# Feed-forward up projections with tokens on the partitions of their sums, and the hidden values transposed for the down projection

## The chip, the cores and the metric

One core of a Trainium2 chip runs the whole program. The metric is the device time of one execution in microseconds, as the median of three runs. The engines are named as in the profile: PE is TensorE (its matmuls; PEld are its loads of the stationary operand), DVE is VectorE, ACT is ScalarE, POOL is GpSimd, SP is SyncE, which issues the weight loads.

## The reference

A trunk of two layers on 256 tokens of width 2048, all in float32. Layer 0 has a recurrent mixer (a matrix memory beside a gated linear recurrence), layer 1 a dilated attention of 16 heads. Each layer ends with the block that this case is about; the hidden width is 5632.

```python
def rmsnorm(x, g):
    y = xf * lax.rsqrt(jnp.mean(jnp.square(xf), axis=-1, keepdims=True) + RMS_EPS)
    return (y * g.astype(jnp.float32)).astype(x.dtype)

def swiglu(h, w1, w3, w2):
    return (jax.nn.silu(h @ w1) * (h @ w3)) @ w2
...
        h = rmsnorm(x, f_norm[l])
        x = x + swiglu(h, f_w1[l], f_w3[l], f_w2[l]).astype(x.dtype)
    return rmsnorm(x, final_norm)
```

## The kernel before, in words

**Exact products out of parts.** Every float32 operand is written as the sum of two parts of type float32r: the rounded value, made by an ACT copy, and the rest, made by a DVE subtraction (`split2` for results, `emit_split` for weights, lines 204 and 205). A product takes three of the four products of parts: high by high, high by low, low by high.

**The weight stream.** All weights come in items of 1 MB, [128, 4, 512], loaded by SP into four buffers `raw`. Each item makes two steps of [128, 2, 512], that is of eight blocks of 128 x 128 weights. For each step ACT writes `wh` and DVE `wl`, four buffers each, three steps (AHEAD) ahead of the products. `emit_step` issues the products of one step to PE, then lets the background tasks run one turn (`run_tasks`). An evacuation (the handling of a finished sum) is a generator in the list `urgent`, which is advanced by one `yield` in every turn. `lag()` waits one turn more (LAG = 1), so that operands made by other engines are there when PE gets to the instruction.

**Two forms of product.** In the *narrow* form (`add_chunk`, `narrow`, lines 272 to 274) the activations are the stationary operand and the weights stream: for each block of 128 features and each of two tiles of 128 tokens there are three matmuls of 512 columns, one for each pair of parts, into a bank `acc` of [128 tokens, 512 outputs]. A step has two feature blocks, so 12 matmuls; a chunk of 512 outputs takes two banks. In the *wide* form (`add_blocks`, lines 294 and 295) the weights are stationary and the activations stream: for each block of 128 x 128 weights one matmul of 512 columns (the high weights by both parts of 256 tokens side by side) and one of 256 columns (the low weights by the high activations). Its sum, [128 outputs, 512], takes one bank, whose two halves `join` adds; units of 128 outputs come in pairs.

**Norms.** The residual `xres` has tokens on the partitions. `norm_evac` adds a chunk of a projection to it, takes the squares, transposes it with PE (`transpose`, line 141, tile `nT`) and writes `xT`, [feature, token] in two parts, times the norm's gains. The norm's own factors, one per token, are applied to the results: `cur["rstd"]` has them for tokens on the partitions; `rstd_rows` spreads them along the free axis into `rb` by two products with ones (line 331), which wide results need.

**The feed-forward block** (`ffn`, lines 921 to 981). The hidden width is 44 blocks of 128, done in two parts (`UPS`): 24 blocks and their down projection, then 20 and theirs. The up projections are wide; units of w1 and w3 alternate. For each block, `up1` joins the w1 sum, multiplies it by `rb` and takes Silu; `up3` joins the w3 sum, multiplies it by `rb` and by the other, and splits the result into the tile `hT`, [hidden, token], four blocks to a tile of the slots. An up stretch is thus 96 or 80 steps. The down projection is narrow, with `hT` as the stationary operand: four chunks of outputs, each over all the hidden blocks of the part.

**Memory.** PSUM: four banks `acc`, two `tp` for transposes, two `mx`. SBUF: six buffers `ev` of [128, 512], eight slots of 8 KB (`hT`, the residual, the attention's tiles, the final gains), used in turn. POOL issues the few other loads and takes the norms' powers; the load of the final gains (`load_fg`) is issued 90 steps before the end.

Of the kernel before, what the change touches and what calls it, by code (L numbers as in the profile page):

```python
# [16 lines left out]
S = 256  # L17
# [19 lines left out]
# buffers: weights as loaded, their float32r parts and how many steps these run ahead  # L37
# [3 lines left out]
# work tiles of 8, 2 and 4 KB per partition  # L41
# [4 lines left out]
# background tasks at a time; stages that a product waits after its operands are issued  # L46
CONC = 3
LAG = 1
# products on constants that bring the tensor engine to its full clock before the data is there
WARM = 13  # L50
# step of the weights' parts from which the first norm is taken up
RS0 = 9
# column groups of the first layer's input projection, in the order of their products
# [11 lines left out]
def trunk_kernel(ctx: ExitStack, tc: tile.TileContext, a, out):  # L65
# [42 lines left out]
    def lag():  # L108
        """For operands of other engines to be ready when the tensor engine gets there."""
        for _ in range(LAG):  # L110
            yield

    def take():
        """One task at a time keeps a bank of mx (and one of tp) from stage to stage."""
        while held["mx"]:
            yield
        held["mx"] = True
# [11 lines left out]
    # ---------------------------------------------------------------- consts  # L129
# [16 lines left out]
    # ------------------------------------------------------ the weight stream  # L146
# [4 lines left out]
    def load_xT(k0, n):  # L151
        """Feature blocks of the transposed input, [feature, token]."""
        i, r = divmod(k0, 8)
        if i not in x_in:
            x_in[i] = slot((8, S), name="xin")
        SP.dma_start(x_in[i][:, r:r + n, :], a["xT"][:, k0:k0 + n, :])
# [34 lines left out]
    def emit_split(s):  # L191
        """Weights of step s into float32r parts."""
        st = steps[s]
        it = st["item"]
        raw = loaded[it][:, 2 * st["half"]:2 * st["half"] + 2, :]
        hi = whp.tile([P, 2, CW], F32R, tag="wh", name="wh")
        lo = wlp.tile([P, 2, CW], F32R, tag="wl", name="wl")
        for k in (0, 1) if s < 2 else (slice(0, 2),):
            if s < 2:
                use_xT(2 * s + k)  # L200
            elif s < KB // 2:
                use_xT(2 * s)
                use_xT(2 * s + 1)
            A.copy(hi[:, k], raw[:, k])  # L204
            V.tensor_tensor(lo[:, k], raw[:, k], hi[:, k].bitcast(F32), op=ALU.subtract)  # L205
        splits[s] = (hi, lo)
        if st["last_half"]:
            loaded.pop(it)
            emit_load()

    def add_unit(src, ch, kb0, first, last, act):
        """Four blocks of features by 512 outputs; tokens on the outputs' partitions."""
        items.append(wload(src, len(items)))
        it = len(items) - 1
        for h in range(2):
            steps.append({
                "item": it, "half": h, "last_half": h == 1, "ch": ch, "kb": kb0 + 2 * h, "act": act,
                "first": first and h == 0, "last": last and h == 1, "wide": False, "before": None,
            })
# [7 lines left out]
    def add_blocks(units):  # L227
        """Units of 128 outputs on the outputs' partitions: (weights, act, evac), two at a time."""
        for i in range(0, len(units), 2):
            pair = []  # L230
            for src, act, evac in units[i:i + 2]:
                items.append(wload(src, len(items)))
                pair.append((len(items) - 1, Chunk(evac), act))
            for h in range(2):
                for it, ch, act in pair:
                    steps.append({
                        "item": it, "half": h, "last_half": h == 1, "ch": ch, "kb": 8 * h, "act": act,
                        "first": h == 0, "last": h == 1, "wide": True, "before": None,
                    })
# [65 lines left out]
    # ------------------------------------------------------------- shared bits  # L305
# [5 lines left out]
    def split2(dst, src):  # L311
        """Exact float32r parts of src into dst [.., 2, S]."""
        A.copy(dst[:, 0, :], src)  # L313
        V.tensor_tensor(dst[:, 1, :], src, dst[:, 0, :].bitcast(F32), op=ALU.subtract)  # L314

    def join(acc, dst):
        """Both column halves of a wide unit's sum, times the tokens' norm factors."""
        A.copy(dst, acc[:, S:])  # L318
        V.tensor_tensor(dst, acc[:, :S], dst, op=ALU.add)  # L319

    def rstd_rows(r):
        """The norm factors along the free axis on every partition."""
# [15 lines left out]
    def norm_evac(n, gains, ssq, xt, last=False):  # L338
        """Adds the chunk to the residual; its transpose, times the gains, for the next products."""

        def gen(ch):
# [35 lines left out]
            if n == NCD - 1:  # L377
                r = const.tile([P, 2], F32, name=f"rstd{gains}")
                V.tensor_reduce(r, ssq, axis=mybir.AxisListType.X, op=ALU.add)
                V.tensor_scalar(r, r, 1.0 / D, EPS, op0=ALU.mult, op1=ALU.add)  # L380
                power(r, r, 2)
                yield
                yield from rstd_rows(r)
                cur["rstd"] = r
                flags.add(f"rstd{gains}")
# [11 lines left out]
    # ================================================================ layer 0  # L397
    # ---- recurrent block: conv, gates and scans in [channel, time]
# [44 lines left out]
    def rg_scan(c, wt):  # L443
        """Two channel blocks, both directions."""
# [18 lines left out]
        # 1 - a^2 = tanh(-log a) (1 + a^2)  # L463
# [50 lines left out]
    # ---- matrix memory: both directions in their quadratic form  # L514
    ml, ys = {}, {}

    def gates_task():
# [39 lines left out]
        # log sigmoid of the forget gates beside softplus(-lam): min(z, 0) - ln(1 + exp(-|z|))  # L557
# [8 lines left out]
        # half of -8 softplus(-lam) = 8 log sigmoid(lam)  # L566
# [6 lines left out]
        # cumulated forget gates, [token, direction * head]  # L573
# [57 lines left out]
    def qk_block(i, h):  # L631
        """q (i = 0, scaled) or k of a head, [feature, token]."""
# [174 lines left out]
    # the residual, two tiles of two chunks  # L807
# [8 lines left out]
    # ================================================================ layer 1  # L816
    at = {}

    def att_qk(i, h):
        """Minus the scaled q (i = 0) or k of a head, [feature, token], in float32r parts."""  # L820
# [38 lines left out]
    def mm3(o, lhs, rhs, start, stop):  # L859
        """One product of float32 operands out of their float32r parts."""  # L860
# [59 lines left out]
    # ==================================================================== ffn  # L920
    def ffn(l, gains, nxt):
# [3 lines left out]
        def up1(f):  # L925
            def gen(ch):
                st["e", f] = e = ev("up")
                while f"rstd{gains}" not in flags:
                    yield
                t = e[:, :S]  # L930
                join(ch.acc[0], t)
                ch.acc = None
                V.tensor_tensor(t, t, cur["rB"], op=ALU.mult)  # L933
                A.activation(t, t, AF.Silu)  # L934
                flags.add(f"up{l}_{f}")
# [4 lines left out]
        def up3(f, f0):  # L940
            def gen(ch):
                while f"up{l}_{f}" not in flags:
                    yield
                e = st.pop(("e", f))
                t = e[:, S:]
                join(ch.acc[0], t)
                ch.acc = None
                V.tensor_tensor(t, t, cur["rB"], op=ALU.mult)
                if (f - f0) % 4 == 0:
                    st["h", f] = slot((4, 2, S), F32R, name="hT")  # L950
                V.tensor_tensor(t, t, e[:, :S], op=ALU.mult)  # L951
                split2(st["h", f - (f - f0) % 4][:, (f - f0) % 4], t)
                flags.add(f"h{l}_{f}")
                yield

            return gen

        def act_h(kb):
            until(f"h{l}_{kb}")
            return st["h", kb // 4 * 4][:, kb % 4]  # L960

        for hidx, (c0, c1) in enumerate(UPS):
            units = []
            for f in range(4 * c0, 4 * c1):
                units += [(a["w1"][l, f], act, up1(f)), (a["w3"][l, f], act, up3(f, 4 * c0))]
            add_blocks(units)
# [16 lines left out]
    # ============================================================ the program  # L983
# [21 lines left out]
    def first_rstd():  # L1005
        """The input's sums of squares, out of its transpose."""
# [47 lines left out]
    def out_proj(w, gains, act, name, order):  # L1054
        """The first two chunks leave the operands that come last for later."""
# [42 lines left out]
    # ------------------------- the last products and the final norm, by tokens  # L1098
# [26 lines left out]
# ---- layout on the host  # L1125
def tiled(w):
    """[K, N] into [N / 512, K / 512, 128, 4, 512]: one contiguous piece per load."""
# [4 lines left out]
def blocks(w):  # L1132
    """[2048, N] into [N / 128, 128, 4, 512]: all the rows of 128 outputs per load."""
# [8 lines left out]
def constants():  # L1142
    """What depends on the shapes alone."""
# [13 lines left out]
def arrange(x, e_norm, e_w_in, e_gate_b, e_conv_w, e_conv_b, e_rg_wa, e_rg_ba, e_rg_wx, e_rg_bx,  # L1157
# [25 lines left out]
        "w1": np.stack([blocks(f_w1[l]) for l in range(2)]),  # L1183
        "w3": np.stack([blocks(f_w3[l]) for l in range(2)]),
# [20 lines left out]
```

## Time and profile before

| what | value |
|---|---|
| median of three runs | 2259.32 us (2259.19 to 2259.65) |
| span of the profiled execution, first to last instruction | 2256.9 us |
| median less span (start and end of an execution) | 2.4 us |
| mean granted TensorE clock over the span | 0.999 |
| PE / PEld busy | 2240.3 / 1903.8 us (99% / 84%) |
| DVE busy | 1391.3 us (62%) |
| ACT busy | 1097.7 us (49%) |
| weights and all else read from HBM | 414.09 MB, 184 GB/s over the span |
| up stretches, layer 0 | 373.84 to 646.49 and 778.90 to 1005.03 us |
| up stretches, layer 1 | 1510.03 to 1782.66 and 1914.98 to 2138.27 us |

The profile is of one execution. Busy time of an engine is the union of its instructions' times; matmuls overlap one another, so a count times a mean duration is more than the busy time, and what one of them costs in a row is the distance from its start to the start of the next. The chain is followed back from the last instruction, at each step to what released it. In rows of groups the columns are the line, engine, operation, output tile and input tiles, shapes and count, then busy time, the mean duration in ns, and the engine's idle time before them with what ended it.

### The profile page before, as it was taken

What the parts mean: (1) busy time and instruction counts of PE and PEld (TensorE: products, weight loads), DVE (VectorE), ACT (ScalarE), POOL (GpSimd) and SP (SyncE); (2) the same over time, 40 slices, a digit from 0 to 9 for tenths busy, and PEclk for the clock granted to TensorE, in tenths of its full rate; (3) what the DMA queues carried; (4) which work ended last, traced back from release to release, by engine and by line L of the source; (5) the groups of instructions that cost most, each with busy time, mean ns of one, the idle gap of its engine ahead of it and who ended that gap; (6) DMA issues with size and microseconds to landing.
All of it is one profiled execution on the core that took longest, in us unless ns stands there. A gap on an engine that the chain in (4) does not pass through costs nothing.

```text
span 2256.9 us, 29286 instructions
## 1 busy us (share of the span) xinstructions
PE 2240.3 (99%) x11660; PEld 1903.8 (84%) x11660; DVE 1391.3 (62%) x1960; ACT 1097.7 (49%) x1603; POOL 23.8 (1%) x42
## 2 busy tenths in 40 slices
PE   9999999999999999999999999999999999999998
PEld 7878888888888888888888888888888888888886
DVE  6867856666654466665566676556666544666654
ACT  5667545444443344444454554454444433444443
POOL 1000000000000000000000000000000000000000
PEclk9999999999999999999999999999999999999999
DMA  7534655555555555555555555445555555555553
GB/s 289 182 122 151 221 171 187 187 187 186 187 186 189 184 187 187 187 193 182 191 190 176 186 183 175 168 171 185 185 187 187 204 187 202 191 189 189 192 196 112
DMA packets 61354, 418.09 MB, mean 185 GB/s; under 512 B 6972, under 2 KB 7628, under 8 KB 12448
## 3 DMA queue, kind: packets, MB, share of 16 engines
q1 hardware_dynamic: 58176, 406.35, 52.1%
q0 software_dynamic: 2608, 9.26, 1.2%
q8 instruction: 91, 1.49, 0.3%
q10 hardware_dynamic: 432, 0.60, 0.1%
q14 instruction: 47, 0.39, 0.0%
HBM read 414.09 MB, written 2.10 MB: 184 GB/s over the span
## 4 chain that ended last, share of the span: by engine, by line
PE 95%; DVE 2%; ACT 1%; issue 1%; DMA 0%; SPq 0%; POOL 0%; POOLq 0%; DVEq 0%; ACTq 0%
PE acc L294 37%; PE acc L295 19%; PE acc L272 12%; PE acc L274 12%; PE acc L273 12%; DVE wl L205 1%; PE rgp L454 1%; ACT wh L204 1%; PE nT L141 0%; DVE xc L421 0%; DMA raw<-in_w_v 0%; PE apT L141 0%; PE num L724 0%; PE asc L862 0%; PE apo L861 0%
## 5 line engine op out<-in xcount | busy, mean ns | idle before, releaser
L205 DVE TENSOR_TENSOR wl<-raw,wh 128x1024 fp32r<-128x1024 f32 (+1 forms) x770 | 932.8, 1221 | 727.2 <-ACT wh L204 698.7
L294 PE MATMUL acc<-xT,wh 128*128 128x512 f32 x3712 | 1314.8, 396 | 0.4 <-ACT v L662 0.4
L204 ACT CAST wh<-raw 128x1024 fp32r<-128x1024 f32 (+1 forms) x770 | 802.0, 1044 | 568.3 <-PE acc L274 324.1
L295 PE MATMUL acc<-xT,wl 128*128 128x256 f32 x3712 | 1045.1, 282 | 0.0
L294 PEld LDWEIGHTS acc<-xT,wh 128*128 128x128 f32 x3712 | 697.8, 188 | 165.5 <-ACT v L662 0.6
L295 PEld LDWEIGHTS acc<-xT,wl 128*128 128x128 f32 x3712 | 696.8, 188 | 1.1 <-DVE wl L205 0.3
L272 PE MATMUL acc<-wh,hT 128*128 128x512 f32 x704 | 276.9, 393 | 0.0
L274 PE MATMUL acc<-wh,hT 128*128 128x512 f32 x704 | 275.9, 392 | 0.0
L273 PE MATMUL acc<-wl,hT 128*128 128x512 f32 x704 | 275.7, 392 | 0.0
L274 PEld LDWEIGHTS acc<-wh,hT 128*128 128x128 f32 x704 | 132.2, 188 | 29.9
L273 PEld LDWEIGHTS acc<-wl,hT 128*128 128x128 f32 x704 | 132.4, 188 | 29.0
L272 PEld LDWEIGHTS acc<-wh,hT 128*128 128x128 f32 x704 | 132.3, 188 | 28.8
L313 ACT CAST hT<-up 128x256 fp32r<-128x256 f32 x88 | 35.8, 406 | 198.7 <-DVE up L951 198.7
L934 ACT ACTIVATE up<-up 128x256 f32<-128x256 f32 x88 | 36.8, 418 | 157.8 <-DVE up L933 157.8
L272 PE MATMUL acc<-wh,xT 128*128 128x512 f32 x256 | 104.1, 407 | 0.5 <-ACT wh L204 0.5
L273 PE MATMUL acc<-wl,xT 128*128 128x512 f32 x256 | 101.3, 396 | 1.0 <-DVE wl L205 1.0
L274 PE MATMUL acc<-wh,xT 128*128 128x512 f32 x256 | 101.1, 395 | 0.0
L319 DVE TENSOR_TENSOR up<-acc,up 128x256 f32<-128x256 f32 x176 | 73.5, 418 | 1.5 <-ACT up L318 1.5
L318 ACT COPY up<-acc 128x256 f32<-128x256 f32 x176 | 64.2, 365 | 0.0
L314 DVE TENSOR_TENSOR hT<-up,hT 128x256 fp32r<-128x256 f32 x88 | 37.4, 426 | 41.6 <-ACT hT L313 41.6
L272 PEld LDWEIGHTS acc<-wh,xT 128*128 128x128 f32 x256 | 48.1, 188 | 12.5 <-ACT wh L204 1.5
L273 PEld LDWEIGHTS acc<-wl,xT 128*128 128x128 f32 x256 | 48.1, 188 | 11.8 <-DVE wl L205 1.6
(228 smaller groups left out, 1371.3 us busy)
## 6 DMA issues: line engine op xcount, KB each, us to landing
raw<-in_w SPq DMA_DIRECT2D x264, 1024.0 KB, 4.8
raw<-in_w_aqk SPq DMA_DIRECT2D x32, 1024.0 KB, 4.9
raw<-in_w_out SPq DMA_DIRECT2D x16, 1024.0 KB, 4.8
raw<-in_w_av SPq DMA_DIRECT2D x16, 1024.0 KB, 4.8
raw<-in_w_o SPq DMA_DIRECT2D x16, 1024.0 KB, 4.8
raw<-in_w_xr SPq DMA_DIRECT2D x8, 1024.0 KB, 8.6
raw<-in_w_qk SPq DMA_DIRECT2D x8, 1024.0 KB, 4.9
raw<-in_w_og SPq DMA_DIRECT2D x8, 1024.0 KB, 4.8
```

The source lines that it names most:

```text
L204: A.copy(hi[:, k], raw[:, k])
L205: V.tensor_tensor(lo[:, k], raw[:, k], hi[:, k].bitcast(F32), op=ALU.subtract)
L272: PE.matmul(acc, xh, hi[:, j, :], start=f, stop=False)
L273: PE.matmul(acc, xh, lo[:, j, :], start=False, stop=False)
L274: PE.matmul(acc, xl, hi[:, j, :], start=False, stop=e)
L294: PE.matmul(acc, wh[:, j, :], x2.rearrange("p a b -> p (a b)"), start=f, stop=False)
L295: PE.matmul(acc[:, :S], wl[:, j, :], x2[:, 0, :], start=False, stop=e)
L313: A.copy(dst[:, 0, :], src)
L314: V.tensor_tensor(dst[:, 1, :], src, dst[:, 0, :].bitcast(F32), op=ALU.subtract)
L318: A.copy(dst, acc[:, S:])
L319: V.tensor_tensor(dst, acc[:, :S], dst, op=ALU.add)
L934: A.activation(t, t, AF.Silu)
```

## The change

Up projections use the narrow form. w1 and w3 are laid out in memory in chunks of 512 outputs as the other narrow weights are (`tiled` in place of `blocks`), and each chunk of w1 is followed by the same chunk of w3. `up1` takes Silu straight out of the two banks, with the norm's factor as the scale of each partition; `up3` multiplies the w3 banks by the factor and by that, in place. The result has tokens on the partitions, in two `ev` tiles of [128, 512]; two turns later 8 PE transposes in two groups of four (tile `hTp`, in the `tp` banks) bring it to [hidden, token], one group in each of two turns, and each group is split into `hT` out of PSUM. The two norms ahead of feed-forward blocks no longer run `rstd_rows`. The names, the down projections, the buffers and the other products stay. Comments and docstrings go as well.

```diff
@@ norm_evac @@
                 power(r, r, 2)
-                yield
-                yield from rstd_rows(r)
                 cur["rstd"] = r
+                if gains == G_O:
+                    yield
+                    yield from rstd_rows(r)
                 flags.add(f"rstd{gains}")
@@ ffn @@
-        def up1(f):
+        def up1(c):
             def gen(ch):
-                st["e", f] = e = ev("up")
                 while f"rstd{gains}" not in flags:
                     yield
-                t = e[:, :S]
-                join(ch.acc[0], t)
+                es = []
+                for t in range(2):
+                    e = ev("up")
+                    A.activation(e, ch.acc[t], AF.Silu, scale=cur["rstd"][:, t:t + 1])
+                    es.append(e)
                 ch.acc = None
-                V.tensor_tensor(t, t, cur["rB"], op=ALU.mult)
-                A.activation(t, t, AF.Silu)
-                flags.add(f"up{l}_{f}")
+                st["e", c] = es
+                flags.add(f"up{l}_{c}")
                 yield
...
-        def up3(f, f0):
+        def up3(c):
             def gen(ch):
-                while f"up{l}_{f}" not in flags:
+                while f"up{l}_{c}" not in flags:
                     yield
-                e = st.pop(("e", f))
-                t = e[:, S:]
-                join(ch.acc[0], t)
+                es = st.pop(("e", c))
+                for t in range(2):
+                    V.scalar_tensor_tensor(
+                        es[t], ch.acc[t], cur["rstd"][:, t:t + 1], es[t], op0=ALU.mult, op1=ALU.mult
+                    )
                 ch.acc = None
-                V.tensor_tensor(t, t, cur["rB"], op=ALU.mult)
-                if (f - f0) % 4 == 0:
-                    st["h", f] = slot((4, 2, S), F32R, name="hT")
-                V.tensor_tensor(t, t, e[:, :S], op=ALU.mult)
-                split2(st["h", f - (f - f0) % 4][:, (f - f0) % 4], t)
-                flags.add(f"h{l}_{f}")
                 yield
+                yield from lag()
+                h = st["h", c] = slot((4, 2, S), F32R, name="hT")
+                for p in range(2):
+                    ps = tp("hTp")
+                    for k in range(2):
+                        f0 = (2 * p + k) * P
+                        for t in range(2):
+                            transpose(ps[:, k, t * P:(t + 1) * P], es[t][:, f0:f0 + P])
+                    A.copy(h[:, 2 * p:2 * p + 2, 0, :], ps)
+                    V.tensor_tensor(
+                        h[:, 2 * p:2 * p + 2, 1, :], ps, h[:, 2 * p:2 * p + 2, 0, :].bitcast(F32), op=ALU.subtract
+                    )
+                    for k in range(2):
+                        flags.add(f"h{l}_{4 * c + 2 * p + k}")
+                    yield
...
         for hidx, (c0, c1) in enumerate(UPS):
-            units = []
-            for f in range(4 * c0, 4 * c1):
-                units += [(a["w1"][l, f], act, up1(f)), (a["w3"][l, f], act, up3(f, 4 * c0))]
-            add_blocks(units)
+            for c in range(c0, c1):
+                add_chunk(a["w1"][l, c], 4, act, up1(c))
+                add_chunk(a["w3"][l, c], 4, act, up3(c))
@@ arrange @@
-        "w1": np.stack([blocks(f_w1[l]) for l in range(2)]),
-        "w3": np.stack([blocks(f_w3[l]) for l in range(2)]),
+        "w1": np.stack([tiled(f_w1[l]) for l in range(2)]),
+        "w3": np.stack([tiled(f_w3[l]) for l in range(2)]),
```

More of the change, by code (lines that the diff above doesn't have):

```diff
@@ L959, in act_h @@
             until(f"h{l}_{kb}")
-            return st["h", kb // 4 * 4][:, kb % 4]
+            return st["h", kb // 4][:, kb % 4]
         for hidx, (c0, c1) in enumerate(UPS):
-            units = []
-            for f in range(4 * c0, 4 * c1):
-                units += [(a["w1"][l, f], act, up1(f)), (a["w3"][l, f], act, up3(f, 4 * c0))]
-            add_blocks(units)
+            for c in range(c0, c1):
+                add_chunk(a["w1"][l, c], 4, act, up1(c))
+                add_chunk(a["w3"][l, c], 4, act, up3(c))
             if hidx == 1:
```

## The prediction

> **What bounds the kernel now.** I read the page first (share of the engines, the chain that ended last, the costliest groups), then the busy time in the four stretches that the change touches, then the chain piece by piece there.
>
> ```profile
> span 2256.9 us, 29286 instructions
> PE 2240.3 (99%) x11660; PEld 1903.8 (84%) x11660; DVE 1391.3 (62%) x1960; ACT 1097.7 (49%) x1603; POOL 23.8 (1%) x42
> ...
> PE 95%; DVE 2%; ACT 1%; issue 1%; DMA 0%; SPq 0%; POOL 0%; POOLq 0%; DVEq 0%; ACTq 0%
> ...
> L205 DVE TENSOR_TENSOR wl<-raw,wh 128x1024 fp32r<-128x1024 f32 (+1 forms) x770 | 932.8, 1221 | 727.2 <-ACT wh L204 698.7
> L294 PE MATMUL acc<-xT,wh 128*128 128x512 f32 x3712 | 1314.8, 396 | 0.4 <-ACT v L662 0.4
> L204 ACT CAST wh<-raw 128x1024 fp32r<-128x1024 f32 (+1 forms) x770 | 802.0, 1044 | 568.3 <-PE acc L274 324.1
> L295 PE MATMUL acc<-xT,wl 128*128 128x256 f32 x3712 | 1045.1, 282 | 0.0
> ```
>
> The reader is to see that TensorE (PE) sets the time: 95% of the chain, and the wide products' lines 294 and 295 hardly ever wait. DVE and ACT mostly wait for each other and for PE to free the buffers of the weights' parts. A time of 396 ns is that of one matmul from start to end; they overlap, so costs here go by start to start. The four up stretches, with the sums of all engines:
>
> ```profile
> core 0: us, PE busy (x) PEld busy (x) DVE busy (x) ACT busy (x) POOL busy (x), PEclk, DMA share, GB/s
> 373.84:646.49 272.65, 272.65 (x1550) 237.71 (x1549) 174.22 (x247) 131.60 (x198) 0.72 (x1) 1.00 0.55 188
> 778.90:1005.03 226.13, 226.13 (x1282) 197.08 (x1281) 143.00 (x198) 106.06 (x157) 0.00 (x0) 1.00 0.55 189
> 1510.03:1782.66 272.63, 272.63 (x1550) 237.60 (x1548) 174.26 (x247) 131.66 (x198) 0.71 (x1) 1.00 0.55 188
> 1914.98:2138.27 223.29, 223.29 (x1281) 195.56 (x1280) 142.90 (x197) 105.64 (x157) 0.00 (x0) 1.00 0.56 191
> sum 994.70, PE 994.70 PEld 867.96 DVE 634.37 ACT 474.97 POOL 1.44; mean PE 248.68 PEld 216.99 DVE 158.59 ACT 118.74 POOL 0.36
> ```
>
> PE is busy in every microsecond of these 994.70 us, at the full clock. They are 96 + 80 + 96 + 80 = 352 steps of 8 weight blocks (128 x 128), 2816 blocks. The second stretch holds products alone: 226.13 / 640 = 353.3 ns a block, one matmul of 512 columns and one of 256, as the chain shows:
>
> ```profile
> 779.76 0.24 PE acc L294
> 780.00 0.12 PE acc L295
> 780.12 0.23 PE acc L294
> ```
>
> So only what changes PE's own work counts, unless PE is made to wait.
>
> **The change, part by part.** *Up products.* A narrow step covers the same 8 blocks with 2 feature blocks x 2 token tiles x 3 matmuls = 12 of 512 columns, 1.5 a block instead of 512 + 256. The columns are equal (768 a block); a quarter of the instructions goes. The products that already do exactly this, with xT as the stationary operand, are those of the first attention group (36 matmuls from 1133.18 on, in the stretch below) and of the next three (23 intervals in each):
>
> ```profile
> 1133.18:1141.58 8.40, 8.40 (x38) 1.00 0.37 125
> 1200.38:1205.74 5.36, 5.36 (x25) 1.00 0.58 196
> 1275.03:1280.39 5.36, 5.36 (x26) 1.00 0.59 196
> 1349.88:1355.26 5.38, 5.38 (x26) 1.00 0.59 196
> ```
>
> (The counts take in one or two that overlap the edges.) 8.40 / 36 = 233.3 ns each; the others give 233.0, 233.0 and 233.9. The same line with hT as the stationary operand isn't always as slow; 24 matmuls on the second and on the third hT tile of a down projection, in its second pass and again in its fourth:
>
> ```profile
> 685.10:690.55 5.45, 5.45 (x26) 1.00 0.53 189
> 690.55:696.15 5.60, 5.60 (x26) 1.00 0.59 202
> 751.30:756.75 5.45, 5.45 (x26) 1.00 0.54 188
> 756.75:762.35 5.60, 5.60 (x26) 1.00 0.55 199
> ```
>
> 227.1 and 233.3 ns, and both come back at the same tile in each pass: the rate goes with the stationary tile, not with chance. The up products' tile is xT, so I take 233.3 ns, and keep 227.1 as the low end. 352 x 12 = 4224 matmuls x 233.3 = 985.5 us.
>
> The Trainium skill, in "TensorE: Matmul & The Clock Gate" (Back-to-back issue gap), gives N / 2.4 + 2.5 ns at full clock, so a fixed cost of 2.5 ns for each matmul; by that half a matmul fewer per block would save an estimated 2816 x 0.5 x 2.5 = 3.5 us in all. The rows above show more for each matmul (233.3 ns for 512 columns), and they decide.
>
> *Transposes.* New on PE: 22 chunks of 512 outputs x 8 = 176 transposes of 128 x 128, in 44 groups of four. The nearest are those of the norm, which also stand between narrow steps (chain; below them eight at the start of an up stretch, and the products of rstd_rows):
>
> ```profile
> 1492.44 0.23 PE acc L274
> 1492.67 0.44 PE nT L141 x4
> 1493.10 0.24 PE acc L272
> ```
>
> ```profile
> 1512.99 0.87 PE nT L141 x8
> ...
> 1522.33 0.44 PE rbp L331 x4
> ```
>
> 44 x 0.44 = 19.4 us, all on the path: PE has no idle time there that could take it. Bounds from other rows of the same operation, and one for a wait of it on DVE:
>
> ```profile
> L141 PE MATMUL nT<-cst,xres x96: 270/272/328, 326.2 to 1513.6; 128*128 128x128 f32 x96
> ...
>   DVE xres L345: 1.2, 4
> ```
>
> Low 0.42 a group (half of 0.87, less a rounding); high 0.44 + 0.30, if each group waited for its input as those four did (1.2 / 4): 32.6 us.
>
> *Norm factors along the rows.* For the two feed-forward norms rstd_rows goes (its wait for the PE broadcast, one DVE copy): the L331 row, 2 x 0.44 = 0.9 us saved.
>
> *The sum.* Before: 994.7, of it 2 x 0.87 norm transposes, which stay. After: 985.5 + 1.7 + 19.4 = 1006.6. Difference +11.9 us.
>
> *Evacuations* (no cost). Beside the weights' parts (352 x 1.221 = 430 us DVE, 352 x 1.044 = 367 ACT, from the groups above) DVE now spends 204 us and ACT 107 on results. Nearest rows to the new operations:
>
> ```profile
> L849 ACT ACTIVATE av<-acc,rstd 128x512 fp32r<-128x512 f32 x8 | 5.0, 682 | 0.0
> L850 DVE SCALAR_TENSOR_TENSOR av<-acc,rstd,av 128x512 fp32r<-128x512 f32 x8 | 5.6, 743 | 0.0
> L313 ACT CAST apv<-apT 128x512 fp32r<-128x512 f32 x16 | 9.4, 585 | 11.8 <-PE apT L141 11.7
> L314 DVE TENSOR_TENSOR apv<-apT,apv 128x512 fp32r<-128x512 f32 x16 | 10.9, 684 | 7.5 <-ACT apv L313 7.5
> ```
>
> A chunk takes 2 x 0.743 + 2 x 0.684 = 2.9 us of DVE and 2 x 0.682 + 2 x 0.585 = 2.5 of ACT; times 22, 63 and 56 us. Both fall, and as neither bounds, this is worth nothing: where one reads 634 us of DVE, 141 go and PE stays.
>
> *New waits.* up3 multiplies in the task turn after the step that follows its last one; the transposes of the first half come two turns later, those of the second three: 2 x 2.80 us in which DVE has to do 2 x 0.743 and its weight parts (1.22 a step). If that cover went, PE would stand before the transpose and the whole queue of products behind it. Then ACT's copy of the transposes waits for PE with the next weight casts behind it; these run three steps (8.4 us) ahead, against 0.585 + 1.04 + 1.22. Nothing.
>
> *Banks, buffers, queues.* A chunk takes two accumulators of four, free again when the next but one begins: 8 steps for evacuations of 1.4 us. The loads are as many and as large; SP issues one for every two steps, now in the order of use, a step being 2.80 instead of 2.83 us: nothing. POOL loses no instruction; its load of the final gains takes its slot one hT tile earlier, so that one tile changes place: 96 matmuls x 6.2 ns, 0.6 us either way.
>
> All of it is against the profiled execution, whose span is 2256.9; the median of the runs, 2259.3, is 2.4 more (start and end, unchanged). **2259.3 + 11.9 = 2271.2 us**, 0.5% slower.
>
> **Rivals.**
> *Quicker products (the other side).* If w1 and w3 as the moving operand meet xT in the quicker pattern of some hT tiles, a matmul takes 227.1: 4224 x 6.2 ns = 26 us less, 2245. It decides from 230.5 ns down (11.9 / 4224 = 2.8 less), where the time is that of before. For it: the fourth stretch above does the second's work in 2.8 us less, so a rhythm can differ with the same tiles. Against: xT is at 233.0 to 233.9 in all four groups. At the middle of the hT tiles, (227.1 + 233.3) / 2 = 230.2, it is no change: 2258.
> *The transposes wait.* 0.30 us in each of 44 groups: +13.2, 2284. For it: those four; against: they had one turn, these have two.
> *Transposes that don't overlap.* At 272 ns each (their whole duration), 176 take 47.9 us instead of 19.4: 2300. Against: 0.44 us for four in the chain. The Trainium skill, same page, Part 4 (PE-mode transpose), speaks of about 275 ns for one in a kernel's context; the trace agrees as to duration (272), not as to spacing (110).
> *It does not do what it says* can't be: the instructions themselves change.
>
> **How the numbers follow.** Forecast 74%: own range 2268 (233.0 ns, 1.3 us less; 0.42 a group, 0.9 less; the one tile's 0.6) to 2275 (233.9 ns, 2.5 more, and the 0.6, rounded up). Quicker products 16%, half of it beyond -0.2%, half between; waiting transposes 8%; not overlapping 2%. A measurement here tells about 0.2% (4.5 us) from no change. So faster 8%, same 8%, slower 84%. The range is 2256 to 2284: down to the middle hT rate with the hT tile's 0.6 and a microsecond of rounding, up to the waiting transposes; the 227.1 case and the last rival stay out.
>
> **What would show it.** Up stretches of 96 steps take about 274.0 us (268.8 + 0.87 + 10 x 0.44) instead of 272.6, those of 80 steps 227.5 (224.0 + 8 x 0.44), and the last two groups of each stand in the down projection behind it; narrow products on xT at 233 ns start to start; 176 hTp transposes in pieces of 0.44 us in the chain; DVE about 1250 us busy, ACT about 1047; no PE wait for es, accumulators or wl. I am wrong if xT's matmuls fall below 231 ns, or if PE stands idle at the chunks' seams.

## The result, and the profile after

The changed kernel takes 2271.28 us (median of five runs, 2270.73 to 2271.55), the kernel before 2259.32 (2258.72 to 2259.65): a ratio of 1.0052, 95% interval 1.0041 to 1.0064. That is 12.0 us slower, where 11.9 were forecast.

The page of the changed kernel, its span, its busy times and its chain:

```profile
span 2269.0 us, 25922 instructions
PE 2251.6 (99%) x10420; PEld 1846.6 (81%) x10420; DVE 1248.0 (55%) x1514; ACT 1042.9 (46%) x1339; POOL 23.8 (1%) x42
...
PE 95%; DVE 2%; ACT 1%; issue 1%; DMA 1%; POOL 0%; POOLq 0%; DVEq 0%; SPq 0%; ACTq 0%
PE acc L272 26%; PE acc L273 26%; PE acc L274 26%; PE acc L294 8%; PE acc L295 4%; PE hTp L141 1%; DVE wl L205 1%; PE rgp L455 1%; ACT wh L204 1%; DMA raw<-in_w_v 1%; PE nT L141 0%; DVE xc L422 0%; PE apT L141 0%; PE num L725 0%; PE asc L863 0%
```

PE is still 95% of the chain. Its instructions fell by 1240 and its time rose; DVE lost 143 us of work and ACT 55, and the time took no notice of either. The four up stretches after, with the same columns as before the change:

```profile
374.24:648.24 274.00, 274.00 (x1201) 221.12 (x1200) 134.02 (x124) 116.53 (x127) 0.72 (x1) 1.00 0.55 185
781.53:1008.99 227.46, 227.46 (x993) 183.62 (x992) 110.06 (x98) 93.55 (x98) 0.00 (x0) 1.00 0.55 185
1514.77:1788.78 274.01, 274.01 (x1202) 220.22 (x1200) 134.07 (x124) 116.45 (x127) 0.71 (x1) 1.00 0.54 185
1922.11:2149.59 227.48, 227.48 (x994) 183.62 (x993) 110.05 (x98) 93.62 (x98) 0.00 (x0) 1.00 0.55 185
sum 1002.95, PE 1002.95 PEld 808.58 DVE 488.20 ACT 420.14 POOL 1.43; mean PE 250.74 PEld 202.15 DVE 122.05 ACT 105.03 POOL 0.36
```

994.70 became 1002.95: 8.2 us more. The first three down projections, after and then before, in one sum each:

```profile
sum 380.33, PE 380.33; mean PE 126.78
```

```profile
sum 377.55, PE 377.55; mean PE 125.85
```

Each takes 0.9 us more, the two groups of transposes of the last chunk ahead of it (2 x 0.44). With the fourth (119.4 after, 118.7 before, from its first product to the end of the span) that is 3.5 us. The rest of the 12.1 us between the spans is at the start: the first long weight load lands a little later (after, then before; pieces of the chain, start, us, what):

```profile
5.26 7.50 DMA raw<-in_w_v
```

```profile
4.97 7.34 DMA raw<-in_w_v
```

In the other runs of either form it lands anywhere from 12.1 to 13.1 us, so this is scatter and not the edited lines; here it is worth 0.4 us.

### The profile page after: what moved, and what is told of

Read it like the earlier page. It is cut to its first block, busy times and chain, and to the rows that moved or that the text cites. A ratio compares the mean times of both kernels' runs of the same rounds, so it can differ in the third digit from the quotient of the medians.

```text
span 2269.0 us, 25922 instructions
## 1 busy us (share of the span) xinstructions
PE 2251.6 (99%) x10420; PEld 1846.6 (81%) x10420; DVE 1248.0 (55%) x1514; ACT 1042.9 (46%) x1339; POOL 23.8 (1%) x42
## 4 chain that ended last, share of the span: by engine, by line
PE 95%; DVE 2%; ACT 1%; issue 1%; DMA 1%; POOL 0%; POOLq 0%; DVEq 0%; SPq 0%; ACTq 0%
PE acc L272 26%; PE acc L273 26%; PE acc L274 26%; PE acc L294 8%; PE acc L295 4%; PE hTp L141 1%; DVE wl L205 1%; PE rgp L455 1%; ACT wh L204 1%; DMA raw<-in_w_v 1%; PE nT L141 0%; DVE xc L422 0%; PE apT L141 0%; PE num L725 0%; PE asc L863 0%
## 5 line engine op out<-in xcount | busy, mean ns | idle before, releaser
L272 PE MATMUL acc<-wh,xT 128*128 128x512 f32 x1664 | 663.8, 399 | 0.9 <-ACT wh L204 0.8
L273 PE MATMUL acc<-wl,xT 128*128 128x512 f32 x1664 | 657.5, 395 | 1.2 <-DVE wl L205 1.2
L274 PE MATMUL acc<-wh,xT 128*128 128x512 f32 x1664 | 657.2, 395 | 0.0
L274 PEld LDWEIGHTS acc<-wh,xT 128*128 128x128 f32 x1664 | 312.4, 188 | 75.9
L272 PEld LDWEIGHTS acc<-wh,xT 128*128 128x128 f32 x1664 | 312.4, 188 | 75.7 <-ACT wh L204 2.0
L273 PEld LDWEIGHTS acc<-wl,xT 128*128 128x128 f32 x1664 | 312.5, 188 | 74.7 <-DVE wl L205 2.2
L294 PE MATMUL acc<-xT,wh 128*128 128x512 f32 x896 | 322.0, 400 | 0.4 <-ACT v L663 0.4
L295 PE MATMUL acc<-xT,wl 128*128 128x256 f32 x896 | 252.2, 281 | 0.0
L294 PEld LDWEIGHTS acc<-xT,wh 128*128 128x128 f32 x896 | 168.5, 188 | 38.9 <-ACT v L663 0.5
L295 PEld LDWEIGHTS acc<-xT,wl 128*128 128x128 f32 x896 | 168.2, 188 | 0.9 <-DVE wl L205 0.3
L964 DVE TENSOR_TENSOR hT<-hTp,hT 128x512 fp32r<-128x512 f32 x44 | 30.4, 691 | 57.1 <-ACT hT L963 57.1
L272 PE MATMUL acc<-wh,oT 128*128 128x512 f32 x128 | 51.0, 398 | 0.0
L274 PE MATMUL acc<-wh,oT 128*128 128x512 f32 x128 | 50.3, 393 | 0.0
```

Of the source, the lines that this page charges most:

```text
L272: PE.matmul(acc, xh, hi[:, j, :], start=f, stop=False)
L273: PE.matmul(acc, xh, lo[:, j, :], start=False, stop=False)
L274: PE.matmul(acc, xl, hi[:, j, :], start=False, stop=e)
L294: PE.matmul(acc, wh[:, j, :], x2.rearrange("p a b -> p (a b)"), start=f, stop=False)
L295: PE.matmul(acc[:, :S], wl[:, j, :], x2[:, 0, :], start=False, stop=e)
L964: V.tensor_tensor(h[:, 2 * p:2 * p + 2, 1, :], ps, h[:, 2 * p:2 * p + 2, 0, :].bitcast(F32), op=ALU.subtract)
```

## Experiments

**What the two terms are worth by themselves.** The transposes are left out.

```diff
-                    ps = tp("hTp")
-                    for k in range(2):
-                        f0 = (2 * p + k) * P
-                        for t in range(2):
-                            transpose(ps[:, k, t * P:(t + 1) * P], es[t][:, f0:f0 + P])
+                    ps = es[p].rearrange("q (k s) -> q k s", k=2)
```

> The changed kernel with the 176 transposes left out: the split into hT reads the two up tiles from SBUF instead of the transposes' bank, so the hidden values are in the wrong places; every other instruction stays. Theory (the two terms of the sum are what was worked out): 44 x 0.44 = 19.4 us less than the changed kernel, 2251.9 us, that is 7.4 us less than before; the up stretches take 269.6 and 224.0 us. Rival (the products themselves are slower in the narrow form by what chunks' seams and evacuations cost, and the transposes fill gaps): less than 10 us go and the time stays above 2259.

Measured: 2251.53 us, ratio to before 0.9967 (0.9955 to 0.9980). Its up stretches (us, PE busy, count, granted clock, DMA share, GB/s):

```profile
374.54:644.21 269.67, 269.67 (x1161) 1.00 0.53 187
776.73:1000.72 223.99, 223.99 (x961) 1.00 0.53 188
1505.72:1775.39 269.67, 269.67 (x1161) 1.00 0.53 187
1907.72:2131.71 223.99, 223.99 (x961) 1.00 0.54 188
sum 987.32, PE 987.32; mean PE 246.83
```

223.99 / 960 = 233.3 ns a matmul, in a stretch of nothing but products. Without its transposes the changed form is therefore quicker than the wide one in the up stretches, by 994.7 - 987.3 = 7.4 us: 0.9 of it is the two `rstd_rows` that went, 6.5 the products. The transposes cost 1002.95 - 987.32 = 15.6 us in the up stretches, which hold 36 of the 44 groups, 0.43 a group. The whole times say the same: 12.0 us above the kernel before with them, 7.4 below it without (2258.92, measured along with this run), so 19.4 us for the 44. Both terms stand as they were worked out, and the rival (transposes in gaps) falls.

**What sets 227 or 233 ns.** The prediction took the rate from the stationary tile, without a reason for it. The places of the tiles in the compiled program suggest one. Bytes within a partition: `xT` begins at 25440, the `wh` buffers at 92192 and every 4096 on, `wl` at 108576 and every 4096, the slots at 137248 and every 8256. The low and the high weights are thus alike modulo 256, and so are all the stationary pieces of one tile (512 bytes apart). The distance (the place of the stationary tile less that of the weights' parts, modulo 256) is 64 for xT; for the hT tiles of the first down projection it is 192, 0, 64, 0, 192, 128. Two tiles are in the prediction (the second, 227.1 ns, at 0; the third, 233.3 ns, at 64); here are the first (192) and the sixth (128), 24 matmuls each, before the change:

```profile
679.60:685.10 5.50, 5.50 (x26) 1.00 0.54 183
707.12:712.70 5.58, 5.58 (x26) 1.00 0.53 186
```

229.2 and 232.5 ns. That gave the theory of the next four runs: the distance decides, 227.1 ns at 0, 233.3 at 64, 232.6 at 128, 229.2 at 192. First 64 bytes behind xT:

```diff
     xT = const.tile([P, KB, 2, S], F32R, name="xT")
+    const.tile([P, 16], F32, name="pad")
```

> The changed kernel with 64 bytes of unused memory a partition behind xT, so that the weights' parts, and all behind them, lie 64 bytes further: the distance from the weights' parts to xT becomes a multiple of 256 bytes (it was 64 more than one). Theory (the rate of a narrow matmul goes with the distance, modulo 256 bytes, of the stationary tile from the weights that stream: 227 ns at 0, 233.3 at 64, 232.6 at 128, 229.2 at 192, as the hT tiles show): xT's matmuls fall to 227 ns; 4224 x 6.3 = 26.6 us from the up products and 768 x 6.3 = 4.8 from the other narrow products on xT, so about 2240 us; the hT tiles keep their rates as they move along. Rival 1 (the rate belongs to the tile's own address): xT has not moved, 233.3 ns and 2271 us, while the hT tiles change their rates. Rival 2 (it belongs to the data or to the stage): nothing changes.

Measured: 2242.26 us, ratio to before 0.9926 (0.9912 to 0.9939), about 29 us less than the changed kernel from a tile that nobody uses.

```profile
372.03:638.99 266.96, 266.96 (x1201) 1.00 0.55 189
772.33:993.90 221.57, 221.57 (x994) 1.00 0.55 189
1498.41:1765.39 266.98, 266.98 (x1201) 1.00 0.55 189
1898.66:2120.23 221.57, 221.57 (x993) 1.00 0.55 190
sum 977.08, PE 977.08; mean PE 244.27
```

An up stretch of 80 steps holds 960 matmuls and 8 groups of transposes: (221.57 - 8 x 0.44) / 960 = 227.1 ns. The second and the third hT tile of the first down projection moved along with the weights' parts and kept their rates, in the second pass 227.1 and 233.3 ns:

```profile
678.52:683.97 5.45, 5.45 (x25) 1.00 0.55 182
683.97:689.57 5.60, 5.60 (x25) 1.00 0.54 195
```

To part the distance from the tile's own address, the unused tile was put ahead of xT, with 48 columns, so that all moved together:

```diff
+    const.tile([P, 48], F32, name="pad")
     xT = const.tile([P, KB, 2, S], F32R, name="xT")
```

> The changed kernel with 192 bytes of unused memory ahead of xT: xT, the weights' parts and all behind them move by 192 bytes, and every distance stays; xT comes to an address that is 32 more than a multiple of 256, as that of the quick hT tile was. Theory (distance): 233.3 ns on xT, 2271 us. Rival 1 (own address): 227 ns on xT, about 2240 us. Rival 2 (data or stage): 2271 us.

Measured: 2271.06 us; the second up stretch:

```profile
781.81:1009.32 227.51, 227.51 (x994) 1.00 0.54 185
```

233.3 ns, as without the edit, though every address moved. The own address is out, and with the run before it the data and the stage are out too. The other two distances (32 and 48 columns behind xT):

> The changed kernel with 128 unused bytes behind xT: distance 192 modulo 256 from the weights' parts to xT, and the slots move along with the weights' parts. Theory (the distance decides, by the table read from the hT tiles): 229.2 ns, 4.1 less for 4224 + 768 narrow products on xT, 20.5 us, so 2250.8. Rival (only distance 0 is quick, all others alike): 2271.

> The changed kernel with 192 unused bytes behind xT: distance 128. Theory: 232.6 ns, 0.7 less for 4992 products, 3.5 us, so 2267.8. Rival (the farther the quicker, half of 256 being the farthest): less than 229 ns, below 2250.

Measured: 2252.36 us at 192 and 2267.22 us at 128; the second up stretch of each:

```profile
777.02:1000.36 223.34, 223.34 (x994) 1.00 0.55 188
```

```profile
779.63:1006.87 227.24, 227.24 (x993) 1.00 0.54 185
```

By the same working 229.0 and 233.0 ns, where the table has 229.2 and 232.6. Both rivals fall: all four distances have their own rate, and 128 is not the quickest.

Two things limit this. At 192 a second rate is on record. In the run without transposes the first hT tile took 233.3 ns in the first pass, right behind an up stretch at 233.3, and 229.2 in the second (24 matmuls each):

```profile
644.21:649.81 5.60, 5.60 (x25) 1.00 0.56 189
677.42:682.92 5.50, 5.50 (x25) 1.00 0.53 188
```

The same is seen in a few first passes of other runs and in no later pass, so what went before has a say too. And the buffers `raw` and `ev`, which ACT and DVE read and write meanwhile, kept their distance from the weights' parts in all of these runs. That the streamed tile is what counts, and not those buffers, is argued and not shown; for it speaks that the spacing in the second up stretch is the same where DVE alone is at work and where ACT alone is (233.3 and 233.3 ns in the changed kernel, 226.8 and 226.7 with the 64 bytes).

The Trainium skill says in "TensorE: Matmul & The Clock Gate" (Step-by-step: what each phase is for) that TensorE reads its streaming operand and the next stationary one through two independent ports, so that the load takes no read bandwidth from the running matmul. The runs here show a spacing that differs by up to 6.2 ns (227.1 and 233.3) with where the tiles lie, for the same instructions. That statement does not lead one to expect this, and the measurement decides; but the runs don't show what it is that the two meet in, or whether it is these two reads.

One attempt to go further: only the low weights moved, by a pool of 64 bytes between the two.

```diff
+    ctx.enter_context(tc.tile_pool(name="gap", bufs=1)).tile([P, 16], F32, name="pad")
     wlp = ctx.enter_context(tc.tile_pool(name="wlp", bufs=SPLIT_BUFS))
```

> The changed kernel with 64 unused bytes between the high and the low weight parts: xT is at distance 64 from the high parts as before and at 0 from the low ones, which one of the three matmuls streams. Theory (a matmul is slow by its own stream's distance from the stationary tile loaded meanwhile): one in three quick, two slow, 231.2 ns on average; 4992 / 3 x 6.3 = 10.5 us less, hT about 0.9 more, so 2261.7. Rival 1 (the three go by the slowest): 2271. Rival 2 (a quick one resets the rhythm of the others): about 2242.

Measured: 2275.31 us, 4 more than the changed kernel; its second up stretch:

```profile
782.55:1011.07 228.52, 228.52 (x994) 1.00 0.53 184
```

234.4 ns on average. The theory and both rivals missed: bringing one of three streams to distance 0 made the three slower, not quicker. The hT tiles, which in that run lie at 0, 64, 128 and 192 from the high parts, took 230.8 to 234.6 ns in the second pass, and the two at 64 from the high and 0 from the low parts, as xT, went at 234.6 and 234.2:

```profile
687.66:693.29 5.63, 5.63 (x26) 1.00 0.55 191
698.83:704.45 5.62, 5.62 (x26) 1.00 0.55 192
```

So the table holds only where high and low weights lie alike modulo 256; the distances from both parts count, or that of the parts from each other, which no run varied by itself. Why any of it matters stays open.

**Does the change lose in any placement?** The kernel before got the same 64 bytes behind xT.

> The kernel before the change with the same 64 bytes behind xT. Theory (distance, for both forms of product, as a fixed cost of each matmul: 227 - 213.3 = 13.7 ns at distance 0, where 512 columns at 2.4 a ns are 213.3): a wide block takes 227 + 120.4 = 347.4 instead of 353.3 ns; 3712 x 5.9 = 21.9 us and 768 x 6.3 = 4.8 from the narrow products on xT, so 2232.6 us. Rival (only a stationary xT minds the distance): 4.8 us less, 2254.5 us, and the changed form would be the faster one at this distance.

Measured: 2249.62 us, ratio 0.9958 (0.9946 to 0.9971), 9.3 us less than where xT lay before, between the two expectations.

```profile
372.09:639.82 267.73, 267.73 (x1549) 1.00 0.56 191
772.23:994.10 221.87, 221.87 (x1282) 1.00 0.56 192
1497.55:1770.21 272.66, 272.66 (x1550) 1.00 0.55 188
1902.53:2128.64 226.11, 226.11 (x1281) 1.00 0.55 189
```

The wide form goes at 221.87 / 640 = 346.7 ns a block in layer 0 and at 353.3 in layer 1, with the same tiles at the same places. Its rate is not set by this distance alone. Two more distances for it, the edits as above:

> The kernel before the change at distance 128 from the weights' parts to xT. What the wide form does with the distance is open: at 64 it took 353.3 ns a block in three stretches and 348.9 in one, at 0 346.7 in two and 353.3 in two. Theory (the wide form has rhythms of its own, not set by the distance): some of the stretches at each of these values, 2245 to 2262 us. Rival (distance): one value in all four stretches.

> The same at distance 192. Theory (rhythms of its own): values of 346.7 to 353.3 ns mixed among the four stretches, 2243 to 2260 us. Rival (distance): one value in all four.

Measured: 2254.62 us at 128 and 2260.72 at 192. At 128 all four stretches run at 351.1 ns and at 192 all four at 353.3 (their second stretches below, over 640 blocks; the 96-step ones, less 1.3 us for transposes and the products of `rstd_rows`, give the same). Here the rival was right and the theory of mixed rhythms wrong:

```profile
776.90:1001.60 224.70, 224.70 (x1281) 1.00 0.55 190
```

```profile
778.46:1004.58 226.12, 226.12 (x1282) 1.00 0.55 189
```

With one value at two distances and two values at the other two, what picks the wide rhythm stays open. So the change loses in some placements and gains in others: it is behind by 12.0 us at 64 and by 12.6 at 128 (2267.22 against 2254.62), ahead by 7.4 at 0 (2242.26 against 2249.62) and by 8.4 at 192 (2252.36 against 2260.72). Last, both forms with the slots brought to distance 0 as well:

```diff
-SLOT = 2064
+SLOT = 2112
```

> The changed kernel with 64 unused bytes behind xT and the slots 8448 bytes apart instead of 8256, so that every hT, oT and y tile, too, is at distance 0. Theory: 227.1 ns on all of them; 2112 x 2.7 (mean 229.8 before) = 5.7 us from hT and 768 x 3.7 = 2.8 from oT and y, below the 2242.3 of the kernel with the 64 bytes alone: 2233.8 us. Rival (the slots were set apart so that other engines' accesses do not meet; the gain is lost in DVE or ACT): 2242 or more.

> The kernel before the change with the same two edits. Theory: the same 8.5 us below the 2249.6 of the kernel before with 64 bytes: 2241 us; the wide stretches may fall in either of the two rhythms seen (346.7 or 353.3 ns a block), which is 1.3 us for 200 blocks, up to 9 either way. With both forms at their best distance the changed form is then ahead by 7 us. Rival (wide at its quick rhythm throughout): about 2231 us, and the changed form is behind.

Measured: the changed form 2234.00 us, ratio to before 0.9890 (0.9876 to 0.9903); the form before with the same two edits 2240.25, ratio 0.9918 (0.9904 to 0.9931). Up stretches of the changed form and then of the wide one:

```profile
sum 977.06, PE 977.06; mean PE 244.26
```

```profile
370.75:638.36 267.61, 267.61 (x1550) 1.00 0.56 191
768.95:995.07 226.12, 226.12 (x1282) 1.00 0.55 189
...
sum 987.45, PE 987.45; mean PE 246.86
```

Here the changed form is the quicker one by 6.2 us (runs of 2233.7 to 2234.4 against 2240.1 to 2240.6 on one chip), in the up stretches by 10.4, and it is the fastest kernel of this study, 25.0 us or 1.1% below the kernel before (2259.03, measured along with it). The wide form had again two rhythms, 346.8 in the stretches of 96 steps and 353.3 in those of 80. Were it at 346.7 throughout, its stretches of 80 steps would take 4.2 us less each, 8.5 in all, and it would be ahead again by 2; no run showed that.

## Why the prediction was right, point by point

*What bounds.* Right: DVE fell to 1248.0 us (about 1250 forecast) and ACT to 1042.9 (1047), and nothing of that reached the time.

*Up products, 233.3 ns.* Right as a size (the run without transposes gives it over 960 matmuls) and right in its rule of thumb, that the rate goes with the stationary tile. Why the rate should stay at 233.3 the prediction didn't argue; it took it over from rows of the same tile, and that this was enough was in part luck. As the runs showed afterwards, the rate goes with where the tile lies to the weights' parts, which the change left as it was; 64 bytes more between them would have put the forecast off by some 26 us (up stretches of 1002.95 against 977.08).

*Transposes, 0.44 us a group of four, all on the path.* Right. The chain of the changed kernel has them as forecast, and no transpose waited for its input: in the view of their tile only ACT and DVE wait, ACT for PE and DVE for ACT.

```profile
428.24 0.23 PE acc L274
428.47 0.44 PE hTp L141 x4
428.91 0.24 PE acc L272
```

```profile
L141 PE MATMUL hTp<-cst,up x176: 270/272/273, 428.3 to 2161.3; 128*128 128x128 f32 x176
...
  PE hTp L141: 85.2, 44
  ACT hT L963: 57.1, 44
```

At 272 ns from start to end and 0.44 us for four they overlap as those of the norm did; the rival of 47.9 us does not hold.

*New waits, banks, queues: nothing.* Right. In the whole kernel the narrow products on xT waited 2.1 us in 1664 times three matmuls (last column), and none of it from the first up stretch on, where the same groups of 1536 each have an idle time of 0.0:

```profile
L272 PE MATMUL acc<-wh,xT 128*128 128x512 f32 x1664 | 663.8, 399 | 0.9 <-ACT wh L204 0.8
L273 PE MATMUL acc<-wl,xT 128*128 128x512 f32 x1664 | 657.5, 395 | 1.2 <-DVE wl L205 1.2
L274 PE MATMUL acc<-wh,xT 128*128 128x512 f32 x1664 | 657.2, 395 | 0.0
```

*The sum.* 274.0 and 227.5 us were forecast for the up stretches, 274.00 and 227.46 measured. What the sum left out is the 0.4 us at the start; with it the spans differ by 12.1 us, the medians of the runs by 12.0.

*Quicker products, 16%.* They did not come, but the rival named a real thing: 64 bytes of placement bring them, and then the change is below the kernel before (2242.26 against 2258.92), as its break-even of 230.5 ns said. With the same 64 bytes the kernel before falls too, to 2249.62, and the change is still ahead.

## What to carry to other kernels

Where TensorE is the bound, take the price of a new form from rows of the same instruction on the same stationary tile, start to start, and add what the form brings along: here a quarter fewer matmuls was worth 6.5 us of 995, and the transposes that it needs took 19.4. Before two forms of product are compared, look at where their operands lie: one unused tile of 64 bytes moved this kernel by 29 us, more than the change itself, and turned the order of the two forms round. And a lighter VectorE and ScalarE, by 143 and 55 us, are worth nothing beside an engine that hardly ever waits.

## What the runs showed of the hardware that was not expected

- A matmul of 512 float32r columns with a fresh stationary tile takes 227.1, 233.3, 233.0 or 229.0 ns from start to start with the stationary tile 0, 64, 128 or 192 bytes modulo 256 behind the streamed weights, high and low alike (up stretches of four runs), and 234.4 on average at 64 from the high and 0 from the low ones. At 192 a hT tile has also gone at 233.3, right behind a stretch at that rate.
- The wide form, 512 and 256 columns with the weights stationary, holds one of several steady rhythms for a whole stretch (346.7, 348.9, 351.1 or 353.3 ns a block), and can hold different ones in two stretches with the same tiles at the same places.
